# A hybrid backbone step whose POOL elementwise work is all given to DVE

## The chip, the cores and the metric

The kernel runs on one core of a Trainium2 chip. Its engines work side by side, each through its own list of instructions in a fixed order: PE multiplies matrices into PSUM, PEld is PE's loading of weights, ACT and DVE do elementwise work on SBUF and PSUM, POOL (GpSimd) does elementwise work on SBUF alone, and SP issues the transfers. The metric is the device time of one launch in microseconds (us).

## The reference, cut to what matters

Two request groups, 512 latent tokens and 128 context tokens, pass through two layers with shared weights. All arithmetic is float32. Per layer, with 1024 channels:

```
mod = silu(c) @ w_ada + b_ada                      # shift, scale, gate: 6 x 1024 per group
h   = rmsnorm(x) * (1 + sc1) + sh1
z   = h @ w_in        # pool u | conv B, C, H | q k v | three gates of 1024
merged = sum over 3 branches of sigmoid(gate_b) * (branch_b @ w_br_b)
x   = x + g1 * (merged @ w_o)
h2  = rmsnorm(x) * (1 + sc2) + sh2
x   = x + g2 * ((silu(h2 @ w_gate) * (h2 @ w_up)) @ w_down)
```

The branches are a centred pooling mixer, a short gated convolution and grouped-query attention (8 query heads, 2 key heads, 64 wide; latent tokens also see 128 cached keys). A last rmsnorm follows layer 2. Outputs are the two token sets and the context keys and values of each layer.

## The kernel before, in words

Channels lie on the 128 partitions, so an activation is 8 chunks of 128 x 640 (512 latent and 128 context columns), and a norm works on two halves of 320 columns. To keep float32 accuracy with the fast number format of PE, every operand is split in two: ACT casts it to a high part (L351 for weights, L924 for normed activations), another engine subtracts that from the exact value to get the low part (L353 on POOL or L355 on DVE for weights, L948 for activations), and each product is three matmuls (hi x hi, lo x hi, hi x lo; L686). Weights come in blocks of 128 x 1024 through four raw buffers (`wr`) and six split buffers (`wq`).

The gate and up projections of hidden blocks 2 to 21 are a Strassen scheme with seven products (L589). It wants four sums of weight quarters, `u` (class Pair, L446, each 128 x 512), four of the normed activations (class Quarters, L544), and adds on the results (L651). `hidden_of` (L1922 to L1929) then makes silu(gate) x up: tanh on ACT, `t * (tanh + 1)` on DVE (L1923), one product in L1926, one in L1929.

A norm (L902 to L948) multiplies each chunk by the reciprocal root (L902), makes the high part on ACT (L924), the exact value on ACT or DVE (L924 or L926) and the low part on DVE (L948), on which PE waits. The root itself is a power on POOL (L885, and L1030 in the head norms of attention). Squares are summed by L849. In layer 1 a background task on DVE multiplies the modulation weights `w_ada` with silu(c): 320 reductions in L756 (`junk`), two for each 256 KB block.

The order of all instructions is not written by hand. A small planner (class _Order) runs the program's tasks as coroutines over engine models when the kernel is built: each operation has a cost per engine, an operation that may run on two engines goes to the one that would end it first, and each engine takes what is due first. `pool`, `dve` and `dve_pool` are those models: DVE 1.04 ns a column plus 75, POOL 2.2 ns a column plus 100. What comes out is one fixed list for each engine; at run time they wait for each other through semaphores alone. The background reductions have the lowest priority and fill what the plan leaves free on DVE.

Of the kernel before, what the change touches and what calls it, by code (L numbers as in the profile page):

```python
# [13 lines left out]
ALU = mybir.AluOpType  # L14
# [200 lines left out]
def tile_backbone(ctx: ExitStack, tc: tile.TileContext, a: dict):  # L215
# [54 lines left out]
    def dve_pool(n, f, **kw):  # L270
        return _Op({"dve": 1.04 * n + 75, "pool": 2.2 * n + 100}, lambda e: f(ENG[e]), bias=BIAS, **kw)
# [78 lines left out]
    def half_split(hi, lo, src, n, back=False):  # L350
        yield act(n, lambda: nc.scalar.copy(hi, src), slack=WEIGHT)  # L351
        if back:
            yield pool(n, lambda: nc.gpsimd.tensor_sub(lo, src, hi), slack=WEIGHT)  # L353
        else:
            yield dve(n, lambda: nc.vector.tensor_sub(lo, src, hi), slack=WEIGHT)  # L355
# [6 lines left out]
    class Unit:  # L362
        def __init__(self, src, n=D, back=False, gate=None, big=False):
            self.src, self.n, self.back, self.gate, self.big = src, n, back, gate, big
            self.loaded, self.ready, self.placed = event(), event(), event()
            self.raw = []
# [5 lines left out]
        def prepare(self, turn):  # L372
# [14 lines left out]
            yield from half_split(self.hi[:, :n], self.lo[:, :n], raw[:, :n], n, self.back)  # L387
# [7 lines left out]
    class Pair:  # L395
# [40 lines left out]
        def sums(self):  # L436
# [3 lines left out]
            for q, x, y, op in (  # L440
# [6 lines left out]
                yield dve_pool(n, f, slack=4.0 * WEIGHT)  # L447
# [13 lines left out]
    BACK_FROM, BACK_M = 2, 0  # L461
# [3 lines left out]
    for l in range(DEPTH):  # L465
# [3 lines left out]
        for i, (n, b) in enumerate(names):  # L469
            gate = go_weights[i] if l == 0 and i < 3 else None  # L470
            plan.append(Unit(a[n][l, b], gate=gate, back=i >= max(BACK_FROM, 3 - 3 * l), big=i == 0))
        MERGE = [(0, 0), (0, 1), (1, 0), (1, 1), (0, 2), (1, 2)]
        MERGE += [(m, b) for m in range(2, KC) for b in range(3)]
        for m, b in MERGE:
            plan.append(Unit(a["w_in"][l, B_G + b * KC + m], back=m < BACK_M and b < 2))
# [29 lines left out]
    class Quarters:  # L505
# [22 lines left out]
        def combine(self):  # L528
# [13 lines left out]
            for q, x, y, _ in steps:  # L542
                for c in (slice(0, 2), slice(2, 4)):
                    yield dve_pool(2 * HA, lambda e: e.tensor_sub(b[q][:, c], b[x][:, c], b[y][:, c]))  # L544
# [273 lines left out]
    class Stats:  # L818
# [15 lines left out]
        def add(self, x, k, half):  # L834
# [6 lines left out]
            else:  # L841
# [6 lines left out]
                else:  # L848
                    f = lambda e: e.tensor_add(self.acc[:, c], self.acc[:, c], sq[:, :n])  # L849
                    yield dve_pool(n, f) if k < KC - 3 else dve(n, lambda: f(nc.vector))  # L850
# [47 lines left out]
    def norm_chunk(l, which, x, k, r, h, c0, n, segs, halves, psum, t_slot, first=None, quarters=None):  # L898
# [149 lines left out]
    def rotary(z, rope):  # L1048
# [10 lines left out]
        yield dve_pool(LAT, lambda e: e.tensor_mul(sw[:, :LAT], sw[:, :LAT], rope.t[:, 1, :LAT]))  # L1059
# [1004 lines left out]
```

## Time and profile before

| | us |
|---|---|
| median of 3 runs | 1954.43 (1951.92 to 1954.71) |
| the profiled execution's own time | 1951.29 |
| its span, first to last instruction | 1949.2 |
| PE busy | 1849.3 (95%) |
| DVE busy | 1460.6 (75%) |
| ACT busy | 795.3 (41%) |
| POOL busy | 307.9 (16%) |
| mean granted TensorE clock | 0.983 |

The busy time of an engine says how much of the span it had an instruction in hand; an instruction that is held up while it runs counts as busy. The chain that ended last is put down to PE for 63% and to DVE for 26% of the span.

### The profile page before, as it was taken

What the parts mean: (1) busy time and instruction counts of PE and PEld (TensorE: products, weight loads), DVE (VectorE), ACT (ScalarE), POOL (GpSimd) and SP (SyncE); (2) the same over time, 40 slices, a digit from 0 to 9 for tenths busy, and PEclk for the clock granted to TensorE, in tenths of its full rate; (3) what the DMA queues carried; (4) which work ended last, traced back from release to release, by engine and by line L of the source; (5) the groups of instructions that cost most, each with busy time, mean ns of one, the idle gap of its engine ahead of it and who ended that gap; (6) DMA issues with size and microseconds to landing.
All of it is one profiled execution on the core that took longest, in us unless ns stands there. A gap on an engine that the chain in (4) does not pass through costs nothing.

```text
span 1949.2 us, 31521 instructions
## 1 busy us (share of the span) xinstructions
PE 1849.3 (95%) x12427; PEld 1806.2 (93%) x12427; DVE 1460.6 (75%) x2529; ACT 795.3 (41%) x1396; POOL 307.9 (16%) x246
## 2 busy tenths in 40 slices
PE   6999999998989999999988999999998999999997
PEld 4889999998979999999988889999998899999997
DVE  7699778888889998997777996333347957768575
ACT  5476622222344242342454675222224534425244
POOL 3333000000341010100135320000004301001011
PEclk9999999999999999999999999999999999999998
DMA  8211144446314434433242100222241122222222
GB/s 303 77 35 40 39 151 158 169 161 227 114 33 133 155 112 159 136 129 107 69 161 60 35 29 33 77 82 76 76 141 55 52 90 76 87 76 79 84 71 71
DMA packets 76533, 195.81 MB, mean 100 GB/s; under 512 B 8801, under 2 KB 12897, under 8 KB 76385
## 3 DMA queue, kind: packets, MB, share of 16 engines
q1 hardware_dynamic: 76386, 193.81, 29.9%
q8 instruction: 97, 1.59, 0.3%
q14 instruction: 50, 0.41, 0.1%
HBM read 186.96 MB, written 5.51 MB: 99 GB/s over the span
## 4 chain that ended last, share of the span: by engine, by line
PE 63%; DVE 26%; issue 5%; DMA 3%; ACT 3%; POOL 1%; SPq 0%; DVEq 0%; ACTq 0%; POOLq 0%
PE ps L686 41%; PE ps L589 16%; DVE junk L756 5%; DVE wq L355 5%; DMA p<-in_w_ada 2%; DVE g L298 1%; PE ps L1209 1%; PE ps L1247 1%; PE ps L1227 1%; DVE u L446 1%; DVE g L301 1%; DVE g L948 1%; DVE st L1215 1%; DVE g L926 1%; PE ps L1682 1%
## 5 line engine op out<-in xcount | busy, mean ns | idle before, releaser
L686 PE MATMUL ps<-g,wq 128*128 128x320 f32 x7488 | 1153.9, 311 | 18.6 <-ACT g L300 10.1
L686 PEld LDWEIGHTS ps<-g,wq 128*128 128x128 f32 x7488 | 1112.7, 189 | 25.8 <-ACT g L300 11.7
L589 PE MATMUL ps<-g,wq 128*128 128x320 f32 x3360 | 502.7, 311 | 16.5 <-DVE z L651 13.9
L589 PEld LDWEIGHTS ps<-g,wq 128*128 128x128 f32 x3360 | 497.1, 189 | 21.1 <-DVE z L651 17.6
L355 DVE TENSOR_TENSOR wq<-wr,wq 128x512 fp32r<-128x512 f32 (+2 forms) x289 | 266.4, 922 | 157.3 <-ACT wq L351 156.1
L351 ACT CAST wq<-wr 128x512 fp32r<-128x512 f32 (+2 forms) x312 | 244.6, 784 | 311.9 <-PE ps L686 228.9
L1534 DVE SCALAR_TENSOR_TENSOR g<-ps,mod,g 128x128 f32<-128x128 f32 (+3 forms) x172 | 83.5, 522 | 120.7 <-PE ps L686 120.5
L756 DVE CUSTOM_DVE_ANT_0 junk<-p,k,vec 128x512 f32<-128x512 f32 x160 | 129.8, 811 | 29.5 <-DMA p<-in_w_ada 26.3
L351 ACT CAST wq<-u 128x512 fp32r<-128x512 f32 x160 | 98.3, 620 | 118.8 <-PE ps L589 61.9
L756 DVE CUSTOM_DVE_ANT_0 junk<-p,k,part 128x512 f32<-128x512 f32 x160 | 124.3, 777 | 19.2 <-DMA p<-in_w_ada 16.6
L355 DVE TENSOR_TENSOR wq<-u,wq 128x512 fp32r<-128x512 f32 x160 | 117.2, 737 | 16.5 <-ACT wq L351 16.5
L1484 ACT ACTIVATE t<-ps 128x640 f32<-128x640 f32 x32 | 22.6, 706 | 197.0 <-PE ps L686 197.0
L446 POOL TENSOR_TENSOR u<-u,wr 128x512 f32<-128x512 f32 x23 | 34.3, 1493 | 404.8 <-DVE u L446 403.4
L849 POOL TENSOR_TENSOR u<-u,t 128x320 f32<-128x320 f32 x11 | 14.8, 1351 | 429.2 <-ACT t L844 429.2
L353 POOL TENSOR_TENSOR wq<-wr,wq 128x1024 fp32r<-128x1024 f32 x23 | 57.6, 2505 | 109.2 <-ACT wq L351 99.2
L686 PE MATMUL ps<-g,g 128*128 128x320 f32 x192 | 46.7, 360 | 21.3 <-DVE g L948 18.6
L1217 ACT ACTIVATE p<-ps,st 128x640 f32<-128x640 f32 x64 | 50.9, 796 | 35.9 <-DVE st L1215 26.3
L924 ACT ACTIVATE g<-t,mod,gain 128x128 fp32r<-128x128 f32 (+4 forms) x96 | 50.9, 576 | 31.9 <-DVE gain L1695 14.6
L298 DVE TENSOR_TENSOR g<-ps,g 128x640 fp32r<-128x640 f32 (+1 forms) x68 | 54.9, 809 | 10.5 <-ACT g L297 9.9
L686 PEld LDWEIGHTS ps<-g,g 128*128 128x128 f32 x192 | 33.4, 212 | 30.1 <-DVE g L948 25.2
L902 POOL TENSOR_TENSOR t<-g,u 128x320 f32<-128x320 f32 (+1 forms) x41 | 53.8, 1320 | 39.8 <-ACT u L970 9.0
L297 ACT CAST g<-ps 128x640 fp32r<-128x640 f32 (+1 forms) x68 | 46.5, 686 | 26.5 <-PE ps L1227 21.9
(172 smaller groups left out, 1702.5 us busy)
## 6 DMA issues: line engine op xcount, KB each, us to landing
p<-in_w_ada SPq DMA_DIRECT2D x160, 256.0 KB, 2.8
wr<-in_w_in SPq DMA_DIRECT2D x76, 512.0 KB, 3.3
wr<-in_w_gate SPq DMA_DIRECT2D x44, 512.0 KB, 3.3
wr<-in_w_up SPq DMA_DIRECT2D x44, 512.0 KB, 3.3
wr<-in_w_down SPq DMA_DIRECT2D x48, 384.0 KB, 3.1
g<-in_w_ada SPq DMA_DIRECT2D x16, 512.0 KB, 7.2
wr<-in_w_br SPq DMA_DIRECT2D x32, 256.0 KB, 2.7
wr<-in_w_o SPq DMA_DIRECT2D x16, 512.0 KB, 4.3
```

Source lines behind the costliest of these rows:

```text
L298: yield dve(n, lambda: nc.vector.tensor_sub(lo, src, hi))
L351: yield act(n, lambda: nc.scalar.copy(hi, src), slack=WEIGHT)
L353: yield pool(n, lambda: nc.gpsimd.tensor_sub(lo, src, hi), slack=WEIGHT)
L355: yield dve(n, lambda: nc.vector.tensor_sub(lo, src, hi), slack=WEIGHT)
L446: f = lambda e: e.tensor_tensor(p[q], p[x], p[y], op=op)
L589: nc.tensor.matmul(out, lhsT=wt[q][:, k * P : k * P + P], rhs=x.get(t, lo, k), start=start and k == 0 and i == 0, stop=stop and k == 3 and ...
L686: nc.tensor.matmul(toks(ps, c0, n), lhsT=wt[:, c], rhs=xt[:, c0 : c0 + n], start=start and i == 0, stop=stop and i == 2,)
L756: return dve(n + 60, lambda: nc.vector.tensor_tensor_reduce(out=waste[:, :n], in0=w, in1=s, scale=0.5, scalar=start, op0=ALU.mult, op1=ALU ...
L902: f = lambda e: e.tensor_mul(t[:, :n], xk, r)
L924: nc.scalar.activation(out, sl, AF.Identity, bias=bias, scale=scale)
L1217: yield act(TOK + 140, lambda: nc.scalar.activation(pp, toks(ps), AF.Exp, bias=st[:, 0:1], accum_out=st[:, 1:2]))
L1534: yield dve(n, lambda: nc.vector.scalar_tensor_tensor(xs, toks(ps, s0, n), mods[l][:, v, seg * KC + m : seg * KC + m + 1], xs, op0=ALU.mul ...
```

## The change: every tensor-tensor operation leaves POOL

An operation that the planner could put on DVE or POOL (`dve_pool`) becomes a plain DVE operation (`dve_any`). Three places that named POOL outright follow: the low part of the input projection's weights (`back`), the product of the first norm (`first`), and two of eight chunks of the last norm. POOL keeps the powers (L885, L1030), memsets and the edges of the pooling sums (L1383).

```
-    def dve_pool(n, f, **kw):
-        return _Op({"dve": 1.04 * n + 75, "pool": 2.2 * n + 100}, lambda e: f(ENG[e]), bias=BIAS, **kw)
+    def dve_any(n, f, **kw):
+        return dve(n, lambda: f(nc.vector), **kw)
...
-    def half_split(hi, lo, src, n, back=False):
+    def half_split(hi, lo, src, n):
         yield act(n, lambda: nc.scalar.copy(hi, src), slack=WEIGHT)
-        if back:
-            yield pool(n, lambda: nc.gpsimd.tensor_sub(lo, src, hi), slack=WEIGHT)
-        else:
-            yield dve(n, lambda: nc.vector.tensor_sub(lo, src, hi), slack=WEIGHT)
+        yield dve(n, lambda: nc.vector.tensor_sub(lo, src, hi), slack=WEIGHT)
...
                 f = lambda e: e.tensor_tensor(p[q], p[x], p[y], op=op)
-                yield dve_pool(n, f, slack=4.0 * WEIGHT)
+                yield dve_any(n, f, slack=4.0 * WEIGHT)
...
         f = lambda e: e.tensor_mul(t[:, :n], xk, r)
-        if first:
-            yield pool(n, lambda: f(nc.gpsimd))
-        else:
-            yield dve(n, lambda: f(nc.vector)) if psum else dve_pool(n, f)
+        yield dve(n, lambda: f(nc.vector))
...
-        if k in (2, 5):
-            yield copied
-            yield pool(n, lambda: nc.gpsimd.tensor_mul(xk, xk, r_sb))
-        else:
-            yield dve(n, lambda: nc.vector.tensor_mul(xk, xk, r_ps))
+        yield dve(n, lambda: nc.vector.tensor_mul(xk, xk, r_ps))
...
-        yield dve_pool(TOK, lambda e: e.scalar_tensor_tensor(t, t, 1.0, c.x, op0=ALU.add, op1=ALU.mult))
+        yield dve_any(TOK, lambda e: e.scalar_tensor_tensor(t, t, 1.0, c.x, op0=ALU.add, op1=ALU.mult))
```

The other uses of `dve_pool` (L446, L544, L849, L1059, L1116, L1179, L1369, L1373, L1495, L1926) change in the same way. The planner then lays out all lists anew. POOL's list shrinks from 251 to 84 instructions, DVE's grows from 2521 to 2651 and ACT's from 1318 to 1355; PE's stays at 12268.

The second half of the norm ahead of layer 2's hidden stage, on DVE. `g` in L948 and L941 is the low part, `t` the product with the root. Before, where POOL makes most products L902:

```order
L926 TENSOR_SCALAR g_14043<-t_14696,gain_77,mod_75 128x128
L926 TENSOR_SCALAR g_14043<-t_14697,gain_77,mod_75 128x192
L948 TENSOR_TENSOR g_14041<-g_14043,g_14038 128x320
L926 TENSOR_SCALAR g_14043<-t_14697,gain_77,mod_75 128x128
L926 TENSOR_SCALAR g_14043<-t_14717,gain_77,mod_75 128x192
L948 TENSOR_TENSOR g_14041<-g_14043,g_14038 128x320
```

The same place after the change (the line numbers are those of the changed file: L898 is the product, L919 the exact value, L941 the low part):

```order
L898 TENSOR_TENSOR t_14729<-g_14036,u_14039 128x320
L919 TENSOR_SCALAR g_14043<-t_14710,gain_77,mod_75 128x128
L919 TENSOR_SCALAR g_14043<-t_14711,gain_77,mod_75 128x192
L941 TENSOR_TENSOR g_14041<-g_14043,g_14038 128x320
L898 TENSOR_TENSOR t_14745<-g_14087,u_14039 128x320
L919 TENSOR_SCALAR g_14043<-t_14729,gain_77,mod_75 128x192
L941 TENSOR_TENSOR g_14041<-g_14043,g_14038 128x320
```

A product joins DVE's list for every chunk, and some of the exact values (here the 128 columns of the middle chunk) go to ACT.

POOL's list in the attention stage of layer 2; `wq<-wr,wq` is a weight's low part, `msz` the power that a head norm waits for. Before:

```order
L353 TENSOR_TENSOR wq_10294<-wr_9903,wq_10293 128x1024
L1030 TENSOR_TENSOR msz_82<-msz_82,mhalf 128x10
L353 TENSOR_TENSOR wq_10333<-wr_9974,wq_10332 128x1024
L1030 TENSOR_TENSOR msz_81<-msz_81,mhalf 128x10
L1116 TENSOR_TENSOR k_10002<-z_10284,k_10001 64x640
L353 TENSOR_TENSOR wq_10426<-wr_10033,wq_10425 128x1024
L1030 TENSOR_TENSOR msz_82<-msz_82,mhalf 128x10
```

And after, where L1019 is that power:

```order
L1019 TENSOR_TENSOR msz_82<-msz_82,mhalf 128x10
L1019 TENSOR_TENSOR msz_81<-msz_81,mhalf 128x10
L1019 TENSOR_TENSOR msz_82<-msz_82,mhalf 128x10
L1019 TENSOR_TENSOR msz_81<-msz_81,mhalf 128x10
L1019 TENSOR_TENSOR msz_82<-msz_82,mhalf 128x10
```

Nothing stands between the powers any more; the weight's low parts stand in DVE's list.

The end of DVE's list, where the last norm's two halves are scaled (L994 before), before:

```order
L994 TENSOR_TENSOR g_14036<-g_14036,ps_18981 128x320 x3
L994 TENSOR_TENSOR g_14087<-g_14087,ps_18981 128x320 x3
L849 TENSOR_TENSOR u_18725<-u_18725,t_19033 128x320
L1534 SCALAR_TENSOR_TENSOR g_14087<-ps_18958,mod_75,g_14087 128x192
L1534 SCALAR_TENSOR_TENSOR g_14087<-ps_18958,mod_75,g_14087 128x128
L883 TENSOR_SCALAR msn_84<-ps_19065 128x3
```

And after (L983 is the scaling, L845 the sum of squares, L1523 the residual add):

```order
L983 TENSOR_TENSOR g_14036<-g_14036,ps_18981 128x320 x4
L983 TENSOR_TENSOR g_14087<-g_14087,ps_18981 128x320 x4
L845 TENSOR_TENSOR u_18725<-u_18725,t_19033 128x320
L1523 SCALAR_TENSOR_TENSOR g_14087<-ps_18958,mod_75,g_14087 128x192
L1523 SCALAR_TENSOR_TENSOR g_14087<-ps_18958,mod_75,g_14087 128x128
L879 TENSOR_SCALAR msn_84<-ps_19065 128x3
```

Two scalings more stand ahead of the second half's last sum of squares, and two more at the end.

## Rows read from the trace of the kernel before

**Rows 1.** The page: busy time of each engine, share of the span, instructions.

```profile
PE 1849.3 (95%) x12427; PEld 1806.2 (93%) x12427; DVE 1460.6 (75%) x2529; ACT 795.3 (41%) x1396; POOL 307.9 (16%) x246
```

**Rows 2.** Busy time by stretch: start:end, length, engines, clock, DMA share, GB/s.

```profile
0.00:63.00 63.00, 45.79 (x242) 30.98 (x242) 49.15 (x71) 32.14 (x56) 21.44 (x14) 0.95 0.69 256
63.00:236.00 173.00, 165.48 (x1185) 160.80 (x1184) 147.07 (x253) 109.83 (x213) 48.27 (x47) 0.99 0.13 40
...
520.00:585.00 65.00, 53.68 (x331) 50.53 (x330) 58.60 (x87) 34.65 (x63) 29.85 (x23) 0.95 0.12 41
585.00:882.00 297.00, 283.45 (x1880) 278.71 (x1880) 286.36 (x582) 112.07 (x196) 34.16 (x23) 0.99 0.42 138
...
975.00:1030.00 55.00, 49.09 (x307) 47.04 (x306) 43.16 (x85) 28.67 (x59) 20.33 (x15) 0.94 0.43 143
1030.00:1200.00 170.00, 157.24 (x1120) 151.10 (x1119) 146.65 (x244) 107.81 (x210) 48.58 (x49) 0.99 0.13 40
...
1474.00:1538.00 64.00, 53.80 (x332) 50.46 (x330) 58.29 (x86) 34.62 (x63) 30.32 (x23) 0.94 0.13 42
...
1907.00:1949.00 42.00, 30.90 (x202) 30.08 (x202) 21.68 (x50) 18.65 (x39) 6.06 (x7) 0.85 0.21 72
sum 1949.00, PE 1849.25 PEld 1806.16 DVE 1460.58 ACT 795.33 POOL 307.86; mean PE 142.25 PEld 138.94 DVE 112.35 ACT 61.18 POOL 23.68
```

**Rows 3.** Waits of PE: engine, line, releaser, us in total, times, longest.

```profile
PE ps L686 <- DVE g L948: 18.6, 17, 2.3
PE ps L589 <- DVE z L651: 13.9, 12, 3.3
```

**Rows 4.** Costliest groups on POOL, shapes apart: count, busy, mean ns, idle before.

```profile
L353 POOL TENSOR_TENSOR wq<-wr,wq 128x1024 fp32r<-128x1024 f32 x23 | 57.6, 2505 | 109.2 <-ACT wq L351 99.2 <-DVE st L1220 8.8 <-POOL u L1383 0.7
L902 POOL TENSOR_TENSOR t<-g,u 128x320 f32<-128x320 f32 x33 | 37.6, 1144 | 27.1 <-ACT u L970 9.0 <-DVE g L926 6.2 <-ACT g L924 5.6
L446 POOL TENSOR_TENSOR u<-u,wr 128x512 f32<-128x512 f32 x23 | 34.3, 1493 | 404.8 <-DVE u L446 403.4 <-POOL u L446 1.4
L1926 POOL TENSOR_TENSOR t<-t,z 128x320 f32<-128x320 f32 x17 | 24.2, 1424 | 206.7 <-DVE t L1923 203.0 <-DVE gain L764 3.7
```

**Rows 5.** Groups on DVE, shapes apart, same columns.

```profile
L355 DVE TENSOR_TENSOR wq<-wr,wq 128x512 fp32r<-128x512 f32 x168 | 131.0, 780 | 101.2 <-ACT wq L351 100.7
...
L355 DVE TENSOR_TENSOR wq<-wr,wq 128x1024 fp32r<-128x1024 f32 x73 | 89.7, 1229 | 49.5 <-ACT wq L351 48.7
...
L1923 DVE SCALAR_TENSOR_TENSOR t<-t,t 128x640 f32<-128x640 f32 x40 | 46.3, 1157 | 7.2 <-ACT t L1922 7.2
...
L849 DVE TENSOR_TENSOR u<-u,t 128x320 f32<-128x320 f32 x43 | 26.8, 635 | 6.0 <-ACT t L844 5.9
...
L446 DVE TENSOR_TENSOR u<-wr,wr 128x512 f32<-128x512 f32 x23 | 22.9, 996 | 0.0
...
L1495 DVE TENSOR_TENSOR u<-u,t 128x640 f32<-128x640 f32 x26 | 21.4, 824 | 0.5
...
L1926 DVE TENSOR_TENSOR t<-t,z 128x320 f32<-128x320 f32 x23 | 11.3, 492 | 0.8
```

**Rows 6.** Timeline at the entry of layer 2's hidden stage: start, us, engine, operation.

```profile
1514.74 4.14 POOL L544 TENSOR_TENSOR g<-g,g 128x640 f32<-128x640 f32 x2
1515.38 2.06 DVE L355 TENSOR_TENSOR wq<-wr,wq 128x512 fp32r<-128x512 f32 x1
...
1522.29 0.68 DVE L355 TENSOR_TENSOR wq<-u,wq 128x512 fp32r<-128x512 f32 x1
```

**Rows 7.** Chain of waits, start of layer 2's attention: start, us, what.

```profile
1034.72 0.87 POOL wq L353
...
1037.53 2.66 DVE t L1035
...
1049.08 2.83 DVE z L1056
```

**Rows 8.** Timeline of DVE at the end of the run.

```profile
1942.56 2.48 DVE L994 TENSOR_TENSOR g<-g,ps 128x320 f32<-128x320 f32 x6 [2.38 <-ACT u L982]
```

More of the change, by code (lines that the diff above doesn't have):

```diff
@@ L362, in tile_backbone, with __init__ @@
     class Unit:
-        def __init__(self, src, n=D, back=False, gate=None, big=False):
-            self.src, self.n, self.back, self.gate, self.big = src, n, back, gate, big
+        def __init__(self, src, n=D, gate=None, big=False):
+            self.src, self.n, self.gate, self.big = src, n, gate, big
             self.loaded, self.ready, self.placed = event(), event(), event()
@@ L386, in prepare @@
             s, raw = self.raw[0]
-            yield from half_split(self.hi[:, :n], self.lo[:, :n], raw[:, :n], n, self.back)
+            yield from half_split(self.hi[:, :n], self.lo[:, :n], raw[:, :n], n)
             RAW.put(s)
@@ L459, in free @@
             WQ.put(self.slot[q])
-    BACK_FROM, BACK_M = 2, 0
     SHIFT = 2000.0
@@ L470, in tile_backbone @@
             gate = go_weights[i] if l == 0 and i < 3 else None
-            plan.append(Unit(a[n][l, b], gate=gate, back=i >= max(BACK_FROM, 3 - 3 * l), big=i == 0))
+            plan.append(Unit(a[n][l, b], gate=gate, big=i == 0))
         MERGE = [(0, 0), (0, 1), (1, 0), (1, 1), (0, 2), (1, 2)]
@@ L474, in tile_backbone @@
         for m, b in MERGE:
-            plan.append(Unit(a["w_in"][l, B_G + b * KC + m], back=m < BACK_M and b < 2))
+            plan.append(Unit(a["w_in"][l, B_G + b * KC + m]))
             if b != 1:
@@ L543, in combine @@
                 for c in (slice(0, 2), slice(2, 4)):
-                    yield dve_pool(2 * HA, lambda e: e.tensor_sub(b[q][:, c], b[x][:, c], b[y][:, c]))
+                    yield dve_any(2 * HA, lambda e: e.tensor_sub(b[q][:, c], b[x][:, c], b[y][:, c]))
                 split_up.append(spawn(self.parts(q, b[q])))
@@ L849, in add @@
                     f = lambda e: e.tensor_add(self.acc[:, c], self.acc[:, c], sq[:, :n])
-                    yield dve_pool(n, f) if k < KC - 3 else dve(n, lambda: f(nc.vector))
+                    yield dve_any(n, f) if k < KC - 3 else dve(n, lambda: f(nc.vector))
                     TT.put(i)
@@ L1058, in rotary @@
         c = spawn(cosine())
-        yield dve_pool(LAT, lambda e: e.tensor_mul(sw[:, :LAT], sw[:, :LAT], rope.t[:, 1, :LAT]))
+        yield dve_any(LAT, lambda e: e.tensor_mul(sw[:, :LAT], sw[:, :LAT], rope.t[:, 1, :LAT]))
         yield c
@@ L1115, in one @@
                 yield dma(hi[r1, PAST:].bitcast(F32), hi[r0, PAST:].bitcast(F32), follow=True, done=d)
-                yield dve_pool(TOK, lambda v: v.tensor_sub(lo[r0, PAST:], z[r0, :], hi[r0, PAST:]))
+                yield dve_any(TOK, lambda v: v.tensor_sub(lo[r0, PAST:], z[r0, :], hi[r0, PAST:]))
                 yield dma(lo[r1, PAST:].bitcast(F32), lo[r0, PAST:].bitcast(F32))
@@ L1178, in one @@
                 yield act(TOK, lambda: nc.scalar.copy(q[r0, :], z[r0, :]))
-                yield dve_pool(TOK, lambda v: v.tensor_sub(q[r1, :], z[r0, :], q[r0, :]))
+                yield dve_any(TOK, lambda v: v.tensor_sub(q[r1, :], z[r0, :], q[r0, :]))
             for d in [spawn(one(e)) for e in range(2)]:
@@ L1368, in pool_mix @@
         lo, hi = 1, POOLW
-        yield dve_pool(POOLW, lambda e: e.tensor_add(cur[:, lo:hi], u[:, lo:hi], u[:, lo - 1 : hi - 1]))
+        yield dve_any(POOLW, lambda e: e.tensor_add(cur[:, lo:hi], u[:, lo:hi], u[:, lo - 1 : hi - 1]))
         step = 1
@@ L1372, in pool_mix @@
             lo, hi = lo + step, hi - step
-            yield dve_pool(POOLW, lambda e: e.tensor_add(
+            yield dve_any(POOLW, lambda e: e.tensor_add(
                 nxt[r, lo:hi], cur[r, lo - step : hi - step], cur[r, lo + step : hi + step]))
@@ L1495, in gate @@
                 f = lambda e: e.tensor_add(acc, acc, t)
-                yield dve_pool(TOK, f) if b == 1 else dve(TOK, lambda: f(nc.vector))
+                yield dve_any(TOK, f) if b == 1 else dve(TOK, lambda: f(nc.vector))
                 TT.put(i)
@@ L1922, in hidden_of @@
         yield act(TOK, lambda: nc.scalar.activation(t, c.x, AF.Tanh, scale=0.5))
-        yield dve_pool(TOK, lambda e: e.scalar_tensor_tensor(t, t, 1.0, c.x, op0=ALU.add, op1=ALU.mult))
+        yield dve_any(TOK, lambda e: e.scalar_tensor_tensor(t, t, 1.0, c.x, op0=ALU.add, op1=ALU.mult))
         TT.put(c.xslot)
         yield c.c22
-        yield dve_pool(HA, lambda e: e.tensor_mul(t[:, HA:], t[:, HA:], c.y))
+        yield dve_any(HA, lambda e: e.tensor_mul(t[:, HA:], t[:, HA:], c.y))
         ZZ.put(c.yslot)
```

## The prediction

> **What bounds the kernel now.** I read the busy times first: PE has work for 1849.3 of 1949.2 us [rows 1]. That work does not change, so about 100 us of idle PE are all that a change on the other engines can win, and the question is where they lie and who is late there. The table by stretch answers the first part [rows 2]. PE idles 17.2 us at the start (length less PE busy), 7.5 and 12.8 in the two attention stages, 11.3 and 10.2 in the two norms ahead of the hidden stages (520 to 585 and 1474 to 1538), 13.5 in layer 1's hidden stage (585 to 882), 5.9 in the norm between the layers, 11.1 at the end. DVE is the busiest of the others: 0.90 to 0.96 of the time in those two norms and in layer 1's hidden stage. The waits of PE answer the second part: its largest are for L948, the low part of a normed chunk, 18.6 us in 17 waits, and for L651, an addition of the Strassen scheme, 13.9 us in 12 [rows 3]. Both are DVE's. So DVE's time in these stretches, and the latency of a chunk through the norm, decide.
>
> Then I looked at what POOL and DVE do to each other. At 1514.74 POOL computes two activation sums in 4.14 us, and a weight split on DVE that starts in it takes 2.06 us; the same split at 1522.29, with no POOL work beside it, takes 0.68 [rows 6]. In the groups by shape the same mark is on every form that DVE runs with two operands from SBUF. The 128 x 512 split has a mean of 780 ns instead of 680, L1923 1157 where L1495, also 640 columns, has 824, L849 635 where L1926, also 320, has 492, and L446 `wr,wr` 996 where 680 would do [rows 5, 6]. DVE's 75% hold a good deal of time in which it stands blocked by POOL.
>
> **The change part by part.** The lists show 167 operations leaving POOL, all arriving on DVE, and 37 going from DVE to ACT.
>
> What DVE gains in work. The four largest groups are 96 of the 167 and cost POOL 57.6 + 37.6 + 34.3 + 24.2 = 153.7 us [rows 4]. On DVE the same shapes cost 23 x 1.22 + 33 x 0.49 + 23 x 0.68 + 17 x 0.49 = 68 us (durations from the 1024 row, L1926, the free split) [rows 5, 6], that is 0.44 of POOL's time. The other 71 are 8 of 640 columns in L902 and 12 more of 640, 26 of 512 in L446, 11 of 320 in L849 and 14 small ones; at the same durations, 850 ns for three sums of some 660 columns (estimate from the 640 row), they come to about 50. Together 118 us.
>
> What DVE gets back. Count times excess gives 16.8 us for the split, 13.3 for L1923, 6.1 for L849 and 7.3 for L446: 43 us from four forms, the lower bound, since other two-operand forms are stretched too. The upper bound is POOL's whole time, 307.9 [rows 1]. In the example POOL's 4.14 us cost DVE 1.38 in the one split shown, a third [rows 6]; a third of 307.9 is 103, and I take 105. The 37 operations that go to ACT are scalings of attention's probabilities and exact values of the norms, at about half a microsecond 18 us (estimate from the 320 and 640 rows), and ACT has room: 109.83 of 173 us in the fullest long stretch [rows 2]. So DVE's busy time stays about where it is: 1460 + 118 - 105 - 18 = 1455, between 1250 and 1520.
>
> Now the stretches, gain positive:
>
> The norms before the hidden stages, +5 each. In the second half of each norm the products sit on POOL at 1.14 us [rows 4], feed ACT, and hold up the exact values and L948 on DVE. In the new list every chunk has a product (0.49), about 1.25 exact values of 0.3 to 0.4, and L948 (0.49): 1.4 us as durations, 1.2 when the ends that overlap are taken off, against some 1.5 now (1.14 on POOL and what it blocks). Eight chunks a half, two halves, and PE waiting in most of them, make 16 x 0.3 = 4.8; the entry of the hidden stage gets two splits back from 2.06 to 0.68 [rows 6], of which PE's work hides about half. That would be 6; PE's idle time there, 10 to 11, is the cap, and DVE's list is longer by 7 instructions with one stall fewer to blame, so 0 to -3 is the floor. I take 5.
>
> The norm between the layers, +2, and the start, +2. Same loop, nine and eight products. At the start DVE also computes 16 long reductions between the chunks; eight products of 0.82 arrive (6.6) and I expect 8 to 10 us of stretched operations to go. PE is back to back in the later part of that stretch, which hides the rest. Bounds -2 to +6 each.
>
> Attention, +4 for both. On the path at the start of layer 2's attention stand a weight split on POOL in front of a power (0.87 us of it on the chain), a copy of 2.66 us and a product of 2.83 [rows 7]; the copy is one that needs no more than L1495's 0.82, the product is of 512 columns and needs 0.68. Three pieces are 4.8 us. Against it, ten splits of 1.22 per layer enter DVE's list in the middle of the softmax chain: 12 us of work in a DVE that is busy 0.85 [rows 2]. From -8 (half the split time ends up on the path) to +12.
>
> Layer 1's hidden stage, +1. DVE is the bound here: 286.4 of 297 us busy. 23 operations arrive, 16 of L1926 and 7 of L446, 16 x 0.49 + 7 x 0.68 = 12.6 us. A third of POOL's 34.16 us here [rows 2], 11 us, is what DVE gets back. The new order also moves 14 background reductions (0.8 us each) from before the stage's last third to behind it, where PE has cover enough. All that nets to nothing within 2 us. From -12 to +9.
>
> The end, -1. Two scalings more on DVE ahead of the last sum of squares and two more behind it, 2.48 / 6 = 0.41 us each [rows 8]: 0.8 on the chain, and up to 0.8 more that the output transfers partly hide.
>
> The other stretches have no PE idle to speak of, or no POOL work. Sum: 5 + 5 + 2 + 2 + 4 + 1 - 1 = 18 us. The profiled execution's own time is 1951.29, which is 3.1 under the median of the three runs; from the middle between the two, 1953, I get 1935.
>
> [...]
>
> **The rivals.**
>
> Slower: DVE becomes the bound. If the long durations are DVE waiting for something other than POOL, they stay, and the moved work comes on top. [...] Point of decision: hardly any of POOL's time given back. For it speaks that a busy time does not tell blocked from working; against it the pair of 2.06 and 0.68 [rows 6].
>
> No change: what was a stall beside POOL becomes a queue. A weight split or a Strassen sum that POOL did off the path now stands ahead of L948 or L651 on DVE, and what the chain wins it loses again; PE's 1849.3 does not move. Time 1951 to 1957.
>
> More: half of PE's idle goes. If latency through POOL, its queue included, is what makes L948 and L651 late, and the clock, 0.94 to 0.95 in the norms and 0.99 in the long stretches [rows 2], stays up when the gaps close, 45 us go: 1908.
>
> The change doing nothing at all is excluded, since the lists have changed.
>
> **How the numbers follow.** The forecast has 0.64, with a range of its own from 1920 to 1949; more has 0.12, no change 0.13, slower 0.11. The range that should hold the time leaves out most of the slower case and the deep end of "more": 1914 to 1955. About 0.2% either way, 1950.5 to 1958.3, is what a measurement of this kernel can tell from no change. Faster is the forecast and "more", 0.76; same 0.13; slower 0.11.
>
> **What would show it.** Right: the 128 x 512 split, L1923 and L849 fall to 0.68, 0.82 and 0.49 us means; DVE's busy time is within 40 us of 1460 although it has 130 instructions more; PE's waits for L948 fall from 18.6 to under 12; both norm stretches are 4 us or more shorter in PE idle. Wrong: means that stay high with POOL empty, DVE over 1540, PE waiting longer for L651 or for attention's transposes than now, or the gain sitting in stretches that I gave nothing.

## The result, and the profile after

The kernel after takes 1882.55 us (median of four runs, 1881.98 to 1883.48) against 1954.32 for the kernel before beside it: a ratio of 0.9636, 95% interval 0.9619 to 0.9652. It is faster, as forecast, but by 72 us where 18 were forecast, and below the range of 1914 to 1955. The profiled execution has a span of 1880.7 us. Medians here and below are of executions that agree within 0.5%; one execution of a run below, the one with idle reads, took 4579.31 us for no known reason and is left out of its median.

The page's busy times come first; they answer to [rows 1].

```profile
PE 1824.9 (97%) x12427; PEld 1793.5 (95%) x12427; DVE 1412.7 (75%) x2659; ACT 813.9 (43%) x1433; POOL 40.1 (2%) x79
```

The span is 68.5 us shorter. PE idles 44.1 less (99.9 to 55.8), and its busy time, with the same 12427 matmuls, is 24.4 shorter. DVE has 130 instructions more and is busy 47.9 us less.

Next the stretches of [rows 2], with their ends in after where as many matmuls have run as at the ends of before. In the start and in attention the two kernels run their matmuls in different orders, so those ends are uncertain by a few us. Columns as in [rows 2].

```profile
0.00:56.00 56.00, 42.91 (x241) 29.49 (x242) 43.30 (x77) 30.47 (x54) 2.28 (x5) 1.00 0.78 289
56.00:223.00 167.00, 163.43 (x1189) 159.94 (x1188) 145.60 (x258) 118.73 (x227) 15.66 (x33) 1.00 0.15 46
...
358.00:508.00 150.00, 140.75 (x933) 138.90 (x932) 114.29 (x243) 34.30 (x49) 0.29 (x1) 0.98 0.52 172
508.00:563.00 55.00, 50.69 (x330) 48.96 (x330) 50.66 (x99) 35.66 (x68) 1.40 (x2) 0.98 0.14 48
563.00:847.00 284.00, 279.68 (x1881) 277.60 (x1880) 274.96 (x584) 113.00 (x197) 0.00 (x0) 0.99 0.44 139
...
939.00:989.00 50.00, 46.52 (x310) 44.50 (x309) 38.99 (x92) 31.49 (x65) 2.65 (x2) 1.00 0.47 157
989.00:1143.00 154.00, 153.41 (x1120) 150.30 (x1119) 139.33 (x246) 109.48 (x210) 14.41 (x33) 1.00 0.16 48
...
1416.00:1471.00 55.00, 50.69 (x331) 48.93 (x330) 50.66 (x99) 35.69 (x68) 1.48 (x2) 0.98 0.14 49
...
1838.00:1881.00 43.00, 30.76 (x202) 29.94 (x202) 23.49 (x54) 18.65 (x39) 1.70 (x2) 0.85 0.20 68
```

Set against [rows 2], where PE idle is length less PE busy, and the forecast is given as a change of length:

| stretch | length, us | PE idle, us | clock | forecast |
|---|---|---|---|---|
| start | 63 to 56 | 17.2 to 13.1 | 0.95 to 1.00 | -2 |
| attention, layer 1 | 173 to 167 | 7.5 to 3.6 | 0.99 to 1.00 | -4 with layer 2 |
| around the merge, layer 1 (372 to 520) | 148 to 150 | 8.4 to 9.3 | 0.98 to 0.98 | none |
| norm, layer 1 | 65 to 55 | 11.3 to 4.3 | 0.95 to 0.98 | -5 |
| hidden stage, layer 1 | 297 to 284 | 13.5 to 4.3 | 0.99 to 0.99 | -1 |
| norm between the layers | 55 to 50 | 5.9 to 3.5 | 0.94 to 1.00 | -2 |
| attention, layer 2 | 170 to 154 | 12.8 to 0.6 | 0.99 to 1.00 | |
| norm, layer 2 | 64 to 55 | 10.2 to 4.3 | 0.94 to 0.98 | -5 |
| end | 42 to 43 | 11.1 to 12.2 | 0.85 to 0.85 | +1 |

These give 63 of the 68.5 us. The gain sits where the forecast looked for it, but is two to four times the forecast in the start and the norms, five times in attention and thirteen times in the hidden stage; only the end came as forecast. The granted clock holds another part. By the clock records of the two traces PE was busy for 52.4 us at the lower level, a granted clock of 0.5, before and for 20.0 us after. From one matmul to the next it is 267 ns there and 147 at 1.0 (medians, the same in both traces), so by estimate 24 us were lost to the lower level before and 9 after, and 15 of PE's 24 us are matmuls that ran at 0.5 before and at 1.0 now. In the rows of the start and of the norm between the layers the granted clock rises from 0.95 and 0.94 to 1.00. The other 9 us I have not traced.

PE's waits (columns as in [rows 3]): L941 is the L948 of before, L647 would be L651.

```profile
PE ps L870 <- DVE u L845: 9.4, 2, 6.3
PE ps L682 <- ACT g L300: 5.8, 5, 4.2
PE ps L585 <- DVE wq L352: 4.8, 2, 2.4
...
PE ps L682 <- DVE g L941: 0.8, 4, 0.3
```

The wait for the low part of a normed chunk goes from 18.6 to 0.8 us, and L651's 13.9 us are gone from the list. At the top now are the sums of squares of the first norm (6.3 us in one wait, as before) and of the last (3.1), and single operations of the hidden stages.

DVE's groups, shapes apart, in the order of [rows 5] (L352 was L355, L1912 L1923, L845 L849, L443 L446, L1484 L1495, L1915 L1926):

```profile
L352 DVE TENSOR_TENSOR wq<-wr,wq 128x512 fp32r<-128x512 f32 x168 | 115.1, 685 | 100.3 <-ACT wq L351 100.1
...
L352 DVE TENSOR_TENSOR wq<-wr,wq 128x1024 fp32r<-128x1024 f32 x96 | 117.1, 1219 | 49.4 <-ACT wq L351 48.6
...
L1912 DVE SCALAR_TENSOR_TENSOR t<-t,t 128x640 f32<-128x640 f32 x40 | 32.8, 819 | 4.3 <-ACT t L1911 4.3
...
L845 DVE TENSOR_TENSOR u<-u,t 128x320 f32<-128x320 f32 x54 | 25.0, 486 | 5.5 <-ACT t L840 5.4
...
L443 DVE TENSOR_TENSOR u<-wr,wr 128x512 f32<-128x512 f32 x40 | 27.4, 686 | 0.4
...
L1484 DVE TENSOR_TENSOR u<-u,t 128x640 f32<-128x640 f32 x32 | 26.3, 822 | 0.6
...
L1915 DVE TENSOR_TENSOR t<-t,z 128x320 f32<-128x320 f32 x40 | 19.4, 485 | 0.3
```

Each of the prediction's four forms now has the duration that it took from free instances: 780 to 685, 1157 to 819, 635 to 486, 996 to 686 ns. The same place as [rows 6], the entry of layer 2's hidden stage, shows it in single instructions: the activation sums L540 (L544 before) take 0.82 us on DVE, and no split takes longer than 0.68.

```profile
1449.79 0.68 DVE L352 TENSOR_TENSOR wq<-wr,wq 128x512 fp32r<-128x512 f32 x1
1450.39 0.82 DVE L540 TENSOR_TENSOR g<-g,g 128x640 f32<-128x640 f32 x1
```

The chain of waits at the start of layer 2's attention, where [rows 7] had a split on POOL, a copy of 2.66 us and a product of 2.83, is PE alone from 985 to 1012 us. Its two longest pieces there:

```profile
984.94 6.46 PE ps L682 x44
...
1001.45 7.04 PE ps L682 x48
```

The end [rows 8] has two scalings more in a row, 3.27 us where six took 2.48:

```profile
1874.06 3.27 DVE L983 TENSOR_TENSOR g<-g,ps 128x320 f32<-128x320 f32 x8 [2.38 <-ACT u L975]
```

### The profile page after: what moved, and what is told of

Read it like the earlier page. It is cut to its first block, busy times and chain, and to the rows that moved or that the text cites. A ratio compares the mean times of both kernels' runs of the same rounds, so it can differ in the third digit from the quotient of the medians.

```text
span 1880.7 us, 31296 instructions
## 1 busy us (share of the span) xinstructions
PE 1824.9 (97%) x12427; PEld 1793.5 (95%) x12427; DVE 1412.7 (75%) x2659; ACT 813.9 (43%) x1433; POOL 40.1 (2%) x79
## 4 chain that ended last, share of the span: by engine, by line
PE 67%; DVE 20%; DMA 5%; issue 5%; ACT 2%; POOL 0%; SPq 0%; DVEq 0%; POOLq 0%; ACTq 0%
PE ps L682 42%; PE ps L585 17%; DVE junk L752 6%; DVE wq L352 5%; DMA p<-in_w_ada 5%; PE ps L1198 2%; PE ps L1236 2%; PE ps L1216 2%; DVE u L443 1%; DVE g L301 1%; PE ps L1671 1%; DVE u L1484 1%; DVE g L555 1%; DVE t L1912 1%; DVE t L647 1%
## 5 line engine op out<-in xcount | busy, mean ns | idle before, releaser
L352 DVE TENSOR_TENSOR wq<-wr,wq 128x512 fp32r<-128x512 f32 (+2 forms) x312 | 277.8, 890 | 156.4 <-ACT wq L351 155.4
L1523 DVE SCALAR_TENSOR_TENSOR g<-ps,mod,g 128x128 f32<-128x128 f32 (+3 forms) x172 | 83.3, 522 | 115.6 <-PE ps L682 115.4
L752 DVE CUSTOM_DVE_ANT_0 junk<-p,k,vec 128x512 f32<-128x512 f32 x160 | 119.7, 748 | 31.4 <-DMA p<-in_w_ada 28.5
L752 DVE CUSTOM_DVE_ANT_0 junk<-p,k,part 128x512 f32<-128x512 f32 x160 | 119.8, 749 | 17.2 <-DMA p<-in_w_ada 14.2
L352 DVE TENSOR_TENSOR wq<-u,wq 128x512 fp32r<-128x512 f32 x160 | 108.9, 685 | 13.3 <-ACT wq L351 13.2
L642 ACT COPY t<-ps 128x320 f32<-128x320 f32 x80 | 34.2, 427 | 69.5 <-PE ps L585 69.5
L917 ACT ACTIVATE g<-t,mod,gain 128x320 fp32r<-128x320 f32 (+5 forms) x108 | 55.6, 572 | 6.5 <-DVE t L898 3.3
L1204 DVE TENSOR_REDUCE st<-ps 128x1 f32<-128x640 f32 x64 | 52.2, 815 | 3.9 <-PE ps L1198 3.6
L1911 ACT ACTIVATE t<-t 128x640 f32<-128x640 f32 x40 | 29.6, 739 | 45.4 <-DVE t L647 45.2
L1198 PE MATMUL ps<-k,g 128*128 128x320 f32 x256 | 48.9, 313 | 0.2 <-ACT p L1206 0.2
L1216 PE MATMUL ps<-ident,p 128*128 128x128 f32 x320 | 45.7, 273 | 0.6 <-ACT p L1206 0.4
L300 ACT ACTIVATE g<-t 128x640 fp32r<-128x640 f32 x44 | 32.3, 739 | 30.8 <-DVE t L1918 30.8
```

The lines of the kernel that those rows point to most:

```text
L752: return dve(n + 60, lambda: nc.vector.tensor_tensor_reduce(out=waste[:, :n], in0=w, in1=s, scale=0.5, scalar=start, op0=ALU.mult, op1=ALU ...
L917: nc.scalar.activation(out, sl, AF.Identity, bias=bias, scale=scale)
L1198: nc.tensor.matmul(toks(ps, c0, n), lhsT=qs, rhs=kt[:, c0 : c0 + n], start=j == 0, stop=j == 1)
L1204: yield dve(TOK, lambda: nc.vector.tensor_reduce(st[:, 0:1], toks(ps), axis=AX.X, op=ALU.max, negate=True))
L1216: nc.tensor.transpose(pt[:, t * P : t * P + P], pp[:, t * P : t * P + P], ident)
L1523: yield dve(n, lambda: nc.vector.scalar_tensor_tensor(xs, toks(ps, s0, n), mods[l][:, v, seg * KC + m : seg * KC + m + 1], xs, op0=ALU.mul ...
```

## The experiments

All ratios are to the kernel before on the same chip. Gains and losses of a stage come from the profiled executions: the shift between the same matmuls in two traces, read at places where all matmuls around have one and the same shift.

### Which half of the change: the engine, or the lists?

The change does two things at once: it runs operations on another engine, and it gives the planner other prices, from which it makes other lists for every engine. Two runs take them apart. The first keeps the old prices and lists and issues POOL's tensor operations on DVE:

```
-        return _Op({"dve": ..., "pool": 2.2 * n + 100}, lambda e: f(ENG[e]), bias=BIAS, **kw)
+        return _Op({"dve": ..., "pool": 2.2 * n + 100}, lambda e: f(nc.vector), bias=BIAS, **kw)
...
-            yield pool(n, lambda: nc.gpsimd.tensor_sub(lo, src, hi), slack=WEIGHT)
+            yield pool(n, lambda: nc.vector.tensor_sub(lo, src, hi), slack=WEIGHT)
...
```

> The planner keeps its old costs and lays out the old order, but every operation it gives to POOL is issued on DVE at that place. Blocking theory (DVE was held up by POOL's reads of SBUF, and that time comes back): most of the 72 us gain, 1890 to 1920 us. Plan theory (the gain is the new order, laid out under costs that fit): little, 1935 to 1960, since DVE's list is now overfull against the plan. Latency theory (POOL is slow and its queue delays the powers): 1890 to 1920 as well, so this run parts only the plan from the other two.

1920.72 us, ratio 0.9855 (0.9834 to 0.9875): 28 us. That is just outside the 1890 to 1920 of the blocking theory and far from most of the gain, and outside the 1935 to 1960 of the plan theory as well: neither is the whole. With the lists of before, DVE runs 167 operations more in 33 us less of busy time:

```profile
PE 1839.9 (96%) x12427; PEld 1797.3 (94%) x12427; DVE 1427.7 (74%) x2696; ACT 795.5 (41%) x1396; POOL 46.4 (2%) x79
```

This run takes away two things, DVE's stalls and the longer time that POOL took for the same operations (2505 against 1229 ns for a weight split of 1024 columns [rows 4, 5]); how the 28 us divide between them no run shows. The second keeps the new prices and lists and issues on POOL as many operations of each line as before, all but the four scalings of the end:

```
-                yield dve_any(n, f, slack=4.0 * WEIGHT)
+                yield dve_but("S444", n, f, slack=4.0 * WEIGHT)
...
+    def dve_but(site, n, f, **kw):
+        def go():
+            p, i = TO_POOL[site], count[site]
+            count[site] += 1
+            f(nc.gpsimd if i < len(p) and p[i] == "p" else nc.vector)
+
+        return dve(n, go, **kw)
```

> The fourth corner: the lists of after (planned as if all were DVE's), but 163 of the 167 operations issued on POOL, counted off so that each line has on POOL as many as before (the 4 scalings of the end stay on DVE). With the old lists, DVE's issue was worth 1.4% (28 us). If the two parts add up, the new lists alone are worth the other 40: 1908 to 1915, ratio 0.978. If the new lists are good only because nothing in them waits for a slow POOL (they were laid out for operations of a third of the time): 1935 to 1975, ratio above 0.99, and the two parts can't be had apart.

1923.76 us, ratio 0.9866 (0.9849 to 0.9883): 26 us, between the two expectations. So:

| | POOL's share on POOL | on DVE |
|---|---|---|
| old lists | 1 | 0.9855 |
| new lists | 0.9866 | 0.9636 |

Of 71 us (0.0364 x 1950), the engine alone is worth 28, the lists alone 26, and 17 come only with both (give or take 6, by the intervals). The traces say where, in us gained over before:

| | old lists, on DVE | new lists, POOL's share on POOL | both |
|---|---|---|---|
| start and attention, layer 1 | 2.2 | 0.0 | 13.6 |
| norm, layer 1, and the first 15 us behind it | 6.8 | 5.8 | 11.7 |
| hidden stage, layer 1 | 6.1 | 6.8 | 12.1 |
| norm between the layers and attention, layer 2 | 6.4 | 6.2 | 22.3 |
| norm, layer 2, and the first 7 us behind it | 7.4 | 5.3 | 11.2 |

In the norms and the hidden stage the two halves about add up. What neither half has by itself sits in the two stretches with attention. With the new lists on POOL, POOL still holds up DVE, as the splits show (685 in after):

```profile
L375 DVE TENSOR_TENSOR wq<-wr,wq 128x512 fp32r<-128x512 f32 x168 | 126.1, 750 | 103.7 <-ACT wq L373 103.5
L375 DVE TENSOR_TENSOR wq<-u,wq 128x512 fp32r<-128x512 f32 x160 | 124.3, 781 | 12.8 <-ACT wq L373 11.9
```

### How POOL costs: by what it reads, and by its queue

Two runs have the lists of after on PE, DVE and ACT, and add work on POOL whose results nobody uses, at 145 places of the kinds where POOL had work before: behind the norms' high parts and the low parts of projection and Strassen weights. One reads: products of a fresh tile with a scratch tile. The other copies one column, to start at the same time, and then only writes (memsets).

```
+            for c in range(0, n - m + 1, m):
+                nc.gpsimd.tensor_tensor(scr[:, :m], scr[:, :m], src[:, c : c + m], op=ALU.mult)
```

> The changed kernel with the same instruction lists on PE, DVE, ACT and SP, and 145 groups of products on POOL that nobody needs: each reads a tile just made (a normed high part, a projection weight's low part, a Strassen weight's low part) and a scratch tile. Blocking theory: DVE's two-operand means rise again, half-clock stretches return, 1905 to 1935 us. Latency theory and plan theory: nobody waits for these products but the powers behind them, 1880 to 1890.

```
+            nc.gpsimd.tensor_copy(scr[:, 0:1], src[:, 0:1])
+            for _ in range(n // 80):
+                nc.gpsimd.memset(scr, 1.0)
```

> As the run with idle products on POOL, same lists elsewhere, but each group is one column copied from that tile and then memsets of a scratch tile for about as long: POOL is occupied and its queue is as full, but it hardly reads SBUF. Blocking theory, as far as it is reads that block: 1880 to 1890 us, DVE's means as in the changed kernel. If POOL's being occupied (its queue ahead of the powers, or its writes) is what costs: as slow as the products, 1905 to 1935.

Reading: 1970.70 us, ratio 1.0116 (1.0095 to 1.0138), slower than either theory allowed. Writing: 1930.56, ratio 0.9909 (0.9892 to 0.9927), the time of the second alternative with the DVE of the first. The busy times, reading first:

```profile
PE 1857.9 (94%) x12427; PEld 1810.9 (92%) x12427; DVE 1505.8 (76%) x2659; ACT 817.2 (41%) x1433; POOL 372.8 (19%) x422
```

```profile
PE 1841.9 (95%) x12427; PEld 1806.4 (94%) x12427; DVE 1416.4 (73%) x2659; ACT 816.5 (42%) x1433; POOL 404.1 (21%) x1173
```

With 333 us of reading work on POOL the same 2659 DVE instructions are busy 93 us longer; with 364 us of writing work (64 of them the one-column copies), 4. So it is POOL's reads that lengthen DVE's instructions. The hidden stage of layer 1 is 25 us longer than in after with the reads and 2 with the writes. But the writes cost 53 us too (0.0273 x 1950), and the waits of PE in that run say where:

```profile
PE ps L1044 <- ACT t L1040: 18.1, 5, 7.2
PE ps L900 <- POOL msn L895: 10.6, 5, 8.2
```

Both hang on a power, which stands in POOL's queue behind the memsets. That is a second way for POOL to cost time; how much of it the kernel before had is the next question.

### Parts of the change put back

The norm products on POOL again:

```
-        yield dve(n, lambda: f(nc.vector))
+        if first:
+            yield pool(n, lambda: f(nc.gpsimd))
+        else:
+            yield dve(n, lambda: f(nc.vector)) if psum else dve_pool(n, f)
```

> The changed kernel with the norms' product alone (L902 before) back on POOL or DVE as the planner likes, and on POOL in the first norm. Blocking theory: the four norms lose what they won, about 30 of the 72 us: 1905 to 1918 us, DVE's exact values and low parts stretched there, and the half clock back in the norms. Latency theory: the same place, but the low parts keep their 480 ns. Plan theory: no particular place, 1882 to 1900.

1901.66 us, ratio 0.9756 (0.9735 to 0.9778), 23 us lost by the ratios and 17 by the spans of the profiled executions. That is between the ranges of the blocking and the plan theory. The traces decide for blocking: 6 us are lost in each of the start and the norm between the layers and 1 to 2 in each of the norms ahead of the hidden stages; PE waits 15.1 us for the low parts again; these take 565 ns in place of 485, and the exact values of 128 columns 656 in place of 340. So the norms alone return a quarter to a third of the gain.

The hidden stages' work (L446, L544, L1923, L1926 of before) free for POOL again:

```
-                yield dve_any(n, f, slack=4.0 * WEIGHT)
+                yield dve_pool(n, f, slack=4.0 * WEIGHT)
...
-        yield dve_any(HA, lambda e: e.tensor_mul(t[:, HA:], t[:, HA:], c.y))
+        yield dve_pool(HA, lambda e: e.tensor_mul(t[:, HA:], t[:, HA:], c.y))
```

> After, with the work of the hidden stages and the weight sums of the Strassen scheme (L446, L544, L1923, L1926) again free to go to POOL; norms, attention and weight splits stay on DVE. Theory 'a POOL operation that reads lengthens the DVE operation beside it': DVE's means for 512-column splits rise again by 40 to 60 ns, and the hidden stage of layer 1 gets back most of the 9 us it lost, the norm stage ahead of it (L446 and L544 also run there) 2 to 4: 1892 to 1900. Rival 'only what stands ahead of the powers in POOL's queue costs': nothing of this stands in attention, so 1881 to 1886. Rival 'DVE was the bound and has room now': fewer instructions on DVE, so 1876 to 1881.

1897.64 us, ratio 0.9729 (0.9701 to 0.9758), 18 us lost, as the theory of reads had it: 11 in layer 1's hidden stage, 3 in each of the norms ahead. Of the splits of 512 columns, where 40 to 60 ns more were expected, those of weights rise from 685 to 810 ns and those of weight sums to 711. "DVE has room now" is refuted: DVE has 78 instructions less and is busy 1432.6 us, 20 more.

The low parts of the projection weights on POOL again, and the same lists with these 23 issued on DVE:

```
-        yield dve(n, lambda: nc.vector.tensor_sub(lo, src, hi), slack=WEIGHT)
+        if back:
+            yield pool(n, lambda: nc.gpsimd.tensor_sub(lo, src, hi), slack=WEIGHT)
+        else:
+            yield dve(n, lambda: nc.vector.tensor_sub(lo, src, hi), slack=WEIGHT)
```

```
-            yield pool(n, lambda: nc.gpsimd.tensor_sub(lo, src, hi), slack=WEIGHT)
+            yield pool(n, lambda: nc.vector.tensor_sub(lo, src, hi), slack=WEIGHT)
```

> After, with the low parts of the projection weights (23 operations) again on POOL. Theory 'a long POOL operation queued ahead of the powers of the small norms delays them': attention of both layers and the norm between the layers lose 10 to 20 us together, and the waits of PE for L1040 and L895 come up: 1893 to 1905. Theory 'reading neighbours alone': 23 operations of 2.5 us block DVE for about a third of that, 18 us, of which PE's work hides most: 1885 to 1889. Forecast of the prediction's own working (attention +4 for both layers): 1884 to 1888.

> The same lists as the run with the weight splits back on POOL (the planner still prices those splits as POOL's and lays out the other engines' work around that), but the instructions are issued on DVE. If it is POOL's queue and reads that cost, this run goes back to the time of after, 1882 to 1888. If it is the order that the planner lays out around a slow POOL split, it stays within 4 us of the run with the splits on POOL.

On POOL 1900.61 us, ratio 0.9745 (0.9721 to 0.9768); the same lists on DVE 1895.07, ratio 0.9719 (0.9696 to 0.9741), between the two expectations and nearer the second. The time expected by the theory of POOL's queue came, but not its reason: the waits behind the powers stay at 1.6 us in all for each line, and 16 of the 21 us lost stay when the splits run on DVE. The order that the planner lays out around a split that it prices at 2.35 us (2.2 x 1024 + 100 ns) costs more than POOL itself does, 5 us.

Attention's own choices restored; 9 operations go to POOL:

```
-        yield dve_any(LAT, lambda e: e.tensor_mul(sw[:, :LAT], sw[:, :LAT], rope.t[:, 1, :LAT]))
+        yield dve_pool(LAT, lambda e: e.tensor_mul(sw[:, :LAT], sw[:, :LAT], rope.t[:, 1, :LAT]))
...
-                yield dve_any(TOK, f) if b == 1 else dve(TOK, lambda: f(nc.vector))
+                yield dve_pool(TOK, f) if b == 1 else dve(TOK, lambda: f(nc.vector))
```

> After, with attention's own choice between DVE and POOL restored (the rotary product, the low parts of keys and queries, the second sum of the projections); the planner sends 9 operations to POOL, 5 of them in attention. Layer 2's attention became 19.7 us shorter with the change, and the weight splits alone explain 8 to 10 of it. Theory 'these five are the rest': attention of layer 2 gets back 5 to 10 us, 1887 to 1893. Rival 'the rest comes from the balance of DVE and ACT that the new lists have': within 3 us of after, 1879 to 1886.

1884.47 us, ratio 0.9663 (0.9647 to 0.9679), some 5 us lost. The time lies in the rival's range, but the intervals overlap, so it decides little. In the trace attention of layer 2 is 3.5 us longer, less than the 5 to 10 that the five operations were to return. From its first matmul (L1020) on, that stage is 17.7 us shorter in after than in before; the splits (9.6 in the run that has them on POOL) and these operations leave another 4 to 5 us of it unexplained.

Two of the last norm's scalings on POOL again:

```
-        yield dve(n, lambda: nc.vector.tensor_mul(xk, xk, r_ps))
+        if k in (2, 5):
+            yield copied
+            yield pool(n, lambda: nc.gpsimd.tensor_mul(xk, xk, r_sb))
+        else:
+            yield dve(n, lambda: nc.vector.tensor_mul(xk, xk, r_ps))
```

> After, with two of the last norm's six scalings on POOL again, as before. There is nothing else on POOL and little on DVE but the other four. The end of before was shorter than that of after by 1.7 us, so if the two scalings are its cause: 1880.5 to 1881.5, faster than after by 1 to 2 us. If a reading POOL stretches DVE's four beside it by as much as it takes off: 1882 to 1883.

1880.10 us, ratio 0.9642 (0.9619 to 0.9665), not to be told from after. In the traces the end is 0.8 us shorter, a little under the expected 1 to 2 and less than the device times can show.

### What a price alone does

Two runs change one number of the planner in that last kernel. Through the new prices six operations and three go from one engine to another, none of them to or from POOL.

```
-        return _Op({"dve": 1.04 * n + 75}, lambda e: f(), **kw)
+        return _Op({"dve": 1.04 * n + 150}, lambda e: f(), **kw)
```

> The run with two final scalings on POOL, with one number of the planner changed: a DVE operation is priced at 1.04 n + 150 ns in place of 75, near what the trace of after shows (512: 685 against 607 by the old price, 640: 820 against 741, 320: 484 against 408). Nothing moves to POOL. Theory 'the order laid out from prices decides as much as the engine does': the time moves by more than 5 us, to the better if truer prices give a better order: 1865 to 1878. Rival 'with POOL empty the lists are near enough, the engine's own order follows what is ready': 1877 to 1885.

```
-        return dve(n + 60, lambda: nc.vector.tensor_tensor_reduce(
+        return dve(n + 190, lambda: nc.vector.tensor_tensor_reduce(
```

> The same with the price of the background reductions alone raised, from n + 60 to n + 190 columns (670 to 805 ns for 512 columns; the trace has 748 + 82 ns for the read of the result). These 336 operations fill DVE in layer 1's hidden stage and around the merge, where PE still waits for L300 and L352. By the theory of prices: the stages from 297 to 557 us lose 2 to 5 us of PE's idle time, 1874 to 1878. By the rival: 1879 to 1882.

The price of plain DVE operations raised: 1912.50 us, ratio 0.9802 (0.9787 to 0.9818), 31 us worse than the kernel with the two scalings. That truer prices give a better order is refuted as a rule. The reductions' price alone: 1866.77, ratio 0.9571 (0.9552 to 0.9590), 13 us better than after, more than the 1874 to 1878 expected, and the fastest of all runs. In the trace 11 of the 17 us by which its span is shorter are gained between 290 and 500 us. The stretch between the 8th and the 24th gating of a branch (L1489 of before), in the kernel with the two scalings first, then with the price too:

```profile
296.00:455.00 159.00, 155.98 (x1058) 154.84 (x1056) 126.86 (x273) 36.75 (x48) 0.00 (x0) 1.00 0.48 163
```

```profile
292.00:443.00 151.00, 151.00 (x1032) 151.00 (x1031) 125.95 (x268) 36.86 (x49) 0.00 (x0) 1.00 0.49 170
```

PE has no idle time left there (3 us before), and 26 matmuls of the stretch, some 4 us, have moved to another place. The same number in the kernel before:

> Before, with nothing changed but the planner's price of the background reductions (n + 60 to n + 190 columns), which took 13 us off on top of the change. If that price is worth the same with or without POOL's share: 1934 to 1942, ratio 0.990 to 0.996. If the order of the lists is what each price happens to make of it: anywhere from 1925 to 1975, and a part of the 72 us is the order's luck, not the engine's.

1928.22 us, ratio 0.9892 (0.9873 to 0.9911): 21 us from one price, with five operations fewer on POOL (241 against 246). With that price on both sides the change is worth 0.9571 / 0.9892 = 0.9675, some 63 us: the change does not live on one accident of the lists, but single orders are worth 20 to 30 us either way.

## Why the prediction was right in sign and short by 52 us

**Right: DVE stands blocked beside POOL.** The means fell to the durations foretold, and the two runs with idle work show the cause: DVE is busy 93 us longer beside products on POOL and 4 longer beside memsets and one-column copies. The small power below did not hold DVE up, as far as its span in the profile tells: it runs for 2.41 us on POOL in after, and the three two-operand products beside it take 0.69 to 0.70 us, against means of 0.68 to 0.69 for their lines in the whole run.

```profile
73.55 0.69 DVE L1048 TENSOR_TENSOR t<-t,g 128x512 f32<-128x512 f32 x1
74.16 0.70 DVE L1045 TENSOR_TENSOR z<-z,g 128x512 f32<-128x512 f32 x1
74.89 0.69 DVE L1050 TENSOR_TENSOR z<-z,t 128x512 f32<-128x512 f32 x1
```

```profile
73.64 2.41 POOL L1019 TENSOR_TENSOR msz<-msz,mhalf 128x10 f32<-128x10 f32 x1 [4.13 <-DVE msz L1017]
```

**Mis-sized: what DVE gets back.** "a third of 307.9 is 103, and I take 105" reads half of its own example. The same 4.14 us of POOL held up a second split of before just as long, which the norm's term counts and this one does not:

```profile
1517.37 2.06 DVE L355 TENSOR_TENSOR wq<-u,wq 128x512 fp32r<-128x512 f32 x1
```

Two splits make it two thirds. The trace of after gives 1460.6 + 118 - 18 - 1412.7 = 148, with the prediction's own 118 and 18; the old lists on DVE give 1460.6 + 118 - 1427.7 = 151. That is about half of POOL's time. A better lower bound was at hand in before: the excess of every form over its free duration, not of four forms. With the means of after as free durations it is 111 us for the forms with two tensor inputs and 25 for those with one. Such durations stand in the trace of before itself: half of the 40 instances of L1923 take 826 ns or less, and half of the 32 of L948 in the norms ahead of the hidden stages 479 or less, against means of 1157 and 654, so the excess of most such forms could have been read off.

**Failed: "That work does not change, so about 100 us of idle PE are all that a change on the other engines can win".** PE's busy time fell by 24.4 us, some 15 of them by the clock. The prediction named the clock in its "more" rival without a price of its own. In the norms it even made PE's idle time a cap on the gain; of the 10 and 9 us that these two lost, 3 in each are PE's busy time (53.68 and 53.80 to 50.69), for the same matmuls.

**Failed: "DVE is the bound here ... All that nets to nothing".** The stage's own terms do not net to nothing: 12.6 us arrive, 11 come back, and if the 14 reductions leave the stage, at 0.8 each, they are 11.2, so DVE was to have 9.6 us less to do. It had 11.4 less (286.36 to 274.96), and the stage lost 13. Twelve reductions left it (DVE's time for `junk`, with their number in brackets, before and after):

```profile
585.00:882.00 297.00, 0.00 (x0) 0.00 (x0) 111.77 (x142) 0.00 (x0) 0.99 0.42 138
```

```profile
563.00:847.00 284.00, 0.00 (x0) 0.00 (x0) 96.35 (x130) 0.00 (x0) 0.99 0.44 139
```

With their reads they are some 10 us, so about 14 came back from POOL, a little more than arrived. DVE was busy 0.96 of the stage before and 0.97 after: a share of busy time that contains stalls does not say whether added work fits. The old lists on DVE, where no reduction leaves, gain 6 us here, and the run with this stage's work back on POOL returns 11.

**Failed: "Attention, +4 for both".** It was 22 by the table of stretches. The sum counted three pieces on the chain and then set 12 us of added splits against them. Yet DVE's busy time in layer 2's attention fell from 146.65 to 139.33 us. The price was right for the splits as instructions; the splits put back on POOL's price cost 16 us even when DVE ran them, so what counted was where they stood in the lists.

**Passed over: "The other stretches have no PE idle to speak of, or no POOL work".** Between 372 and 520 us of before PE idled 8.4 us, and POOL was busy for 12.55:

```profile
372.00:520.00 148.00, 139.59 (x931) 137.62 (x931) 120.56 (x246) 34.23 (x49) 12.55 (x8) 0.98 0.54 179
```

The change won nothing there, so the forecast did not suffer. But it is mostly there that the reductions' price later won its 11 us.

**Not in the sum at all: the lists as a term of their own.** The run that comes closest to the forecast's mechanism, DVE unblocked with the order as it was, is the one with old lists on DVE: 28 us, against 18 forecast. The other 43 need the new lists. The working read the new lists for what stands ahead of what at single places and took the planner's effect as neutral for the rest; the price runs show that it moves this kernel by 13 to 31 us with hardly an operation moved between engines. Why the new lists are better as a whole is shown only in part (the splits, the low parts of the norms). The part that needs both halves sits in the stretches with attention, where the splits laid out at POOL's price lost 5 and 10 us on DVE; that points to the splits' places, but no run shows that they are all of it. How much is due to the 37 operations that went from DVE to ACT, and how much to the order alone, stays open.

**The rivals.** "DVE becomes the bound" is refuted by DVE's busy time (1412.7 us after, 1460.6 before). "No change, a queue in place of a stall" is refuted by the waits for L941 (0.8 us, where those for L948 were 18.6). "More", with 0.12, had the right direction and named both the latency and the clock; even its 1908 was 25 us too high.

## What to carry to other kernels

A change of engine under a planner is two changes; run the old lists on the new engine and the new lists on the old one before giving the gain to either. Read an engine's busy share only after taking out what its instructions take longer than their free instances, form by form, since a stalled engine looks full (DVE was busy 0.96 of layer 1's hidden stage of before, and some 14 us of that came back). And where gaps of PE close, count the matmuls at the lower granted clock as part of what can be won (here some 15 of PE's 24 us, by estimate).

## What the runs showed of the hardware that was not expected

- POOL's memsets with one-column copies, 364 us more of them, left DVE's instructions at their durations (1416.4 against 1412.7 us); 333 us of POOL products lengthened them by 93, or 0.28 us for each us on POOL.
- It is not only the two-operand forms that POOL lengthened: the exact values of 128 columns (L926, L919 after), with one tensor input, took 684 ns before, 340 after and 353 with the old lists on DVE. Of the six copies of 128 x 640 (L1035) five took their free 475 to 487 ns before, and one, the piece of 2.66 us in [rows 7], 2648.
- POOL was held up as well: the pooling edges (L1383, L1372 after), 32 of them, took 323 ns each before and 238 after, with nothing changed but the neighbours; with the old lists on DVE they took 364.
